# RMS normalisation of 16 x 1024 x 512 in float32: statistics computed one group ahead, and a first load begun in small transfers

## The chip, the cores and the metric

The kernel runs on one core of one Trainium2 chip. The metric is device time in microseconds (us). The profile's span of one execution is about 1.8 us shorter than that execution's device time. DVE is the vector engine, ACT the scalar engine, and SP the engine that issues the transfers; 16 DMA engines move the data, each transfer in packets. A transfer is said to have landed when the profile shows its completion; each DMA engine ends its share of a transfer with a packet of 4 bytes, the completion record. Timed comparisons were made in rounds on the same chip: the kernel before and the other kernel take turns.

## The reference, cut to what matters

```python
def reference(x, gamma):                     # x: 16 x 1024 x 512 float32
    eps = 1e-5
    rms = np.sqrt(np.mean(x ** 2, axis=-1, keepdims=True) + eps)
    return (x / rms * gamma).astype(np.float32)
```

Each of 16,384 rows of 512 numbers is read once and written once. That is 33.55 MB in and 33.55 MB out, 67.11 MB in all. No row depends on another.

## The kernel before

The rows are cut into four tiles of 128 partitions x 32 rows x 512 columns, 8.39 MB each. Three buffers ("slots") of that size lie in on-chip memory, so the fourth tile must wait until the first one has been stored. Rows are handled in groups of G = 8. ACT squares them and DVE scales them in place. For every second group DVE also sums the squares (`tensor_reduce`); for the others ACT accumulates them itself. All large transfers are issued by SP, in program order, onto one queue.

```python
    load(0, 0, 0, 16)                      # tile, slot, first row, end row
    load(0, 0, 16, 32)
    load(1, 1, 0, 32)
    ...
    def compute(slot, r0, r1):
        for g in range(r0, r1, G):
            ...
            if (g // G) % 2:
                for h in range(0, G, H):   # H = 4
                    sq = psum.tile([P, H, D], fp32, name="sq")
                    nc.scalar.activation(out=sq, in_=slots[slot][:, g + h : g + h + H, :], func=AF.Square)
                    nc.vector.tensor_reduce(out=ss[:, h : h + H], in_=sq, axis=mybir.AxisListType.X, op=OP.add)
            else:
                for r in range(G):
                    nc.scalar.activation(out=sq_scratch, in_=slots[slot][:, g + r, :],
                                         func=AF.Square, accum_out=ss[:, r : r + 1])
            nc.scalar.activation(out=rms, in_=ss, func=AF.Sqrt, bias=eps_t, scale=1.0 / D)
            nc.vector.reciprocal(out=rstd, in_=rms)
            for r in range(G):
                nc.vector.scalar_tensor_tensor(out=slots[slot][:, g + r, :], in0=slots[slot][:, g + r, :],
                    scalar=rstd[:, r : r + 1], in1=gamma_b, op0=OP.mult, op1=OP.mult)

    compute(0, 0, 8)
    store(0, 0, 0, 1)
    load(2, 2, 0, 16)
    store(0, 0, 1, 2)
    load(2, 2, 16, 24)
    store(0, 0, 2, 3)
    load(2, 2, 24, 32)
    compute(0, 8, 32)
    store(0, 0, 3, 32)
    compute(1, 0, 16)
    store(1, 1, 0, 16)
    load(3, 0, 0, 16)                      # waits until tile 0 is stored
    load(3, 0, 16, 32)
    compute(1, 16, 32)
    store(1, 1, 16, 32)
    compute(2, 0, 32)
    store(2, 2, 0, 32)
    compute(0, 0, 16)
    store(3, 0, 0, 16)
    compute(0, 16, 32)
    store(3, 0, 16, 32)
```

## Time and profile before

| | before |
|---|---|
| device time | 162.08 us, median of 3 runs (161.98 to 162.15) |
| span of the profiled execution | 161.0 us |
| DVE, ACT busy | 123.3 us, 79.9 us |
| moved by the main DMA queue | 67.11 MB |
| last store issued, landed | 148.0 us, 160.0 us |

The profiled execution itself took 162.76 us, above all the timed ones. Its trace may be trusted for what happens and in what order, but not for tenths of a microsecond.

These lines are from the profile's page of the kernel before: busy time of the engines, the 40 slices for DVE and the DMA engines, the DMA queue, and the chain that ended last, by engine.

```profile
PE 2.0 (1%) x2; PEld 0.5 (0%) x2; DVE 123.3 (77%) x163; ACT 79.9 (50%) x162; POOL 0.2 (0%) x4
...
DVE  0101909999999509999999999998999999997000
...
DMA  7999999969798999999699999999999699699993
...
q1 hardware_dynamic: 2448, 67.11, 97.4%
...
DVE 70%; ACT 12%; DMA 8%; issue 2%; DVEq 0%
```

Two readings compete here. The chain says that the vector engine bounds the kernel (70% of the span). The DMA queue says that the packets filled 97.4% of the time of all 16 DMA engines. The table of stretches speaks for the second; experiment 2 tests both. Its last two columns are the DMA share and the rate:

```profile
core 0: us, PE busy (x) PEld busy (x) DVE busy (x) ACT busy (x) POOL busy (x), PEclk, DMA share, GB/s
2.00:158.00 156.00, 2.04 (x2) 0.49 (x2) 123.12 (x161) 79.20 (x162) 0.00 (x0) 1.00 1.00 428
13.00:148.00 135.00, 0.00 (x0) 0.00 (x0) 122.43 (x160) 78.61 (x161) 0.00 (x0) 1.00 1.00 431
```

The DMA share is 1.00 for 156 of 161 us. The single digits below 9 in the DMA row need not be holes: shares of single stretches also rise above 1 (1.67 from 20 to 22 us, then 0.23 from 22 to 24), so bytes of a packet seem to be counted in one place, and only longer stretches can be trusted. The Trainium skill, "DMA: Bandwidth & Descriptors", section "Where 436 GB/s comes from", puts the ceiling of the on-chip memory's ports at 435 GB/s; the 431 GB/s of this trace are within 1% of it. "Perfetto Trace Analysis", section "Roofline", says that a core which alone uses its memory can exceed its 358 GB/s share by up to about 20%; here 431 / 358 = 1.20.

The same view restricted to single DMA issues gives the time from issue to landing. First comes the first load, then the last store, both of the kernel before. The times after "x1" are how long the issue took in ns and when it started.

```profile
L42 SPq DMA_DIRECT2D slot<-in_x_dram x1: 383/383/383, 0.7 to 0.7; - x1
...
  ACT sq_scratch L78: 10.4, 1
...
DMA to landing us min/median/max: 12.2/12.2/12.2
...
L45 SPq DMA_DIRECT2D out_dram<-slot x1: 332/332/332, 148.0 to 148.0; - x1
...
DMA to landing us min/median/max: 12.0/12.0/12.0
```

An issue takes 0.3 to 0.4 us, while its data lands 12 us later. ACT waits 10.4 us for the first load. The last store needs 4.19 MB / 431 GB/s = 9.7 us for its data alone, so at 148.0 us hardly anything was queued ahead of it: the vector engine finishes just when the stream runs dry.

These DVE lines from the timeline of the kernel before show the late start and one hole; the columns are start, duration, engine, line, operation:

```profile
24.27 10.67 DVE L87 SCALAR_TENSOR_TENSOR slot<-slot,rstd,gamma_b 128x512 f32<-128x512 f32 x16
...
60.04 0.20 DVE L85 RECIPROCAL rstd<-rms 128x8 f32<-128x8 f32 x1 [5.41 <-ACT rms L84]
```

### The profile page before, as it was taken

The page shows a single profiled execution, that of the slowest core. Times are in us where ns is not written, and L with a number is a line of the kernel's source. Part 1 is how long each engine was busy: PE and PEld are TensorE (multiplying, and loading weights), DVE is VectorE, ACT ScalarE, POOL GpSimd, SP SyncE. Part 2 cuts the span into 40 slices and gives each one's busy share as a digit, 9 for nine tenths or more (in the row PEclk, how much of TensorE's full clock was granted, in tenths as well). Part 3 has the DMA queues.
Part 4 walks back from the last instruction along what each step waited for, and adds up shares of the span by engine and source line. Part 5 has one row for each costly group of instructions (what it writes and reads, how often), then busy time and mean ns, then how long its engine had stood idle before and what let it go on. Part 6 is the DMA issues. An engine that isn't in the chain of part 4 may idle for free.

```text
span 161.0 us, 414 instructions
## 1 busy us (share of the span) xinstructions
PE 2.0 (1%) x2; PEld 0.5 (0%) x2; DVE 123.3 (77%) x163; ACT 79.9 (50%) x162; POOL 0.2 (0%) x4
## 2 busy tenths in 40 slices
PE   3100000000000000000000000000000000000000
PEld 1000000000000000000000000000000000000000
DVE  0101909999999509999999999998999999997000
ACT  3007999930490999999500933003998960000000
POOL 0000000000000000000000000000000000000000
DMA  7999999969798999999699999999999699699993
GB/s 253 399 407 497 399 423 489 521 293 489 326 466 356 466 403 501 460 472 443 297 480 407 415 480 407 407 489 407 407 497 521 277 505 521 269 489 407 407 391 138
DMA packets 2452, 67.13 MB, mean 417 GB/s; under 512 B 273, under 2 KB 273, under 8 KB 658
## 3 DMA queue, kind: packets, MB, share of 16 engines
q1 hardware_dynamic: 2448, 67.11, 97.4%
q14 instruction: 2, 0.02, 0.0%
q10 hardware_dynamic: 2, 0.00, 0.0%
HBM read 33.56 MB, written 33.55 MB: 417 GB/s over the span
## 4 chain that ended last, share of the span: by engine, by line
DVE 70%; ACT 12%; DMA 8%; issue 2%; DVEq 0%
DVE slot L87 51%; DVE ss L73 18%; DMA slot<-in_x_dram 8%; ACT sq_scratch L78 6%; ACT sq L72 4%; DVE rstd L85 1%; ACT L84 1%; ACT rms L84 1%; DVEq L142 0%
## 5 line engine op out<-in xcount | busy, mean ns | idle before, releaser
L87 DVE SCALAR_TENSOR_TENSOR slot<-slot,rstd,gamma_b 128x512 f32<-128x512 f32 x128 | 85.8, 747 | 0.1
L78 ACT ACTIVATE sq_scratch<-slot 128x512 f32<-128x512 f32 x64 | 40.1, 627 | 14.4 <-DMA slot<-in_x_dram 13.1
L73 DVE TENSOR_REDUCE ss<-sq 128x4 f32<-128x2048 f32 x16 | 36.1, 2273 | 10.3 <-ACT sq L72 10.2
L72 ACT ACTIVATE sq<-slot 128x2048 f32<-128x2048 f32 x16 | 29.8, 1865 | 13.9 <-DVE ss L73 13.9
L84 ACT ACTIVATE rms<-ss,eps_t 128x8 f32<-128x8 f32 x16 | 4.5, 298 | 27.9 <-DVE ss L73 27.7
L78 ACT ACTIVATION_READ_ACCUMULATOR sq_scratch<-slot 128x1 f32 x64 | 12.1, 189 | 0.0
L85 DVE RECIPROCAL rstd<-rms 128x8 f32<-128x8 f32 x16 | 2.9, 193 | 9.8 <-ACT rms L84 9.8
L58 DVE COPY gamma_b<-sq 128x512 f32<-128x512 f32 x1 | 0.7, 691 | 3.6 <-PE sq L56 3.6
L56 PE MATMUL sq<-gamma_row,ones_col 1*128 1x512 f32 x2 | 2.0, 1122 | 2.5 <-DMA gamma_row<-in_gamma_dram 2.5
L78 ACT ACT_TABLE_LOAD x1 | 1.3, 1283 | 1.3 <-PEq L131 1.3
L84 ACT ACT_TABLE_LOAD x1 | 1.3, 1283 | 0.0
L54 DVE MEMSET ones_col<- 1x128 f32 x1 | 0.2, 165 | 0.8 <-PEq L131 0.8
L56 PEld LDWEIGHTS sq<-gamma_row,ones_col 1*128 1x128 f32 x2 | 0.5, 305 | 2.5 <-issue 2.5
L131 POOL MEMSET const-bfloat16-1.0<- 128x1 bf16 x1 | 0.1, 103 | 0.0
L131 POOL MEMSET const-uint8-127<- 128x1 uint8 x1 | 0.1, 103 | 0.0
L131 POOL MEMSET const-float32-1.0<- 128x1 f32 x1 | 0.1, 100 | 0.0
L131 POOL MEMSET const-float32-0.0<- 128x1 f32 x1 | 0.1, 99 | 0.2 <-issue 0.2
L61 DVE MEMSET eps_t<- 128x1 f32 x1 | 0.1, 59 | 0.0
## 6 DMA issues: line engine op xcount, KB each, us to landing
slot<-in_x_dram SPq DMA_DIRECT2D x5, 4096.0 KB, 21.5
out_dram<-slot SPq DMA_DIRECT2D x4, 4096.0 KB, 16.5
out_dram<-slot SPq DMA_DIRECT2D x1, 7424.0 KB, 31.9
slot<-in_x_dram SPq DMA_DIRECT2D x2, 2048.0 KB, 34.2
out_dram<-slot SPq DMA_DIRECT2D x3, 256.0 KB, 22.8
gamma_row<-in_gamma_dram ACTq DMA_DIRECT2D x1, 2.0 KB
slot<-in_x_dram SPq DMA_DIRECT2D x1, 40.8
out_dram<-slot SPq DMA_DIRECT2D x1, 23.5
```

Of the source, the lines that this page charges most:

```text
L54: nc.vector.memset(ones_col, 1.0)
L56: nc.tensor.matmul(gamma_psum[:, 0], ones_col, gamma_row, start=True, stop=True)
L58: nc.vector.tensor_copy(out=gamma_b, in_=gamma_psum[:, 0])
L61: nc.vector.memset(eps_t, eps)
L72: nc.scalar.activation(out=sq, in_=slots[slot][:, g + h : g + h + H, :], func=AF.Square)
L73: nc.vector.tensor_reduce(out=ss[:, h : h + H], in_=sq, axis=mybir.AxisListType.X, op=OP.add)
L78: nc.scalar.activation(out=sq_scratch, in_=slots[slot][:, g + r, :], func=AF.Square, accum_out=ss[:, r : r + 1],)
L84: nc.scalar.activation(out=rms, in_=ss, func=AF.Sqrt, bias=eps_t, scale=1.0 / D)
L85: nc.vector.reciprocal(out=rstd, in_=rms)
L87: nc.vector.scalar_tensor_tensor(out=slots[slot][:, g + r, :], in0=slots[slot][:, g + r, :], scalar=rstd[:, r : r + 1], in1=gamma_b, op0=O ...
L131: nc = _bacc.Bacc("TRN2", target_bir_lowering=False, num_devices=1)
```

## The change

The intent is twofold. The statistics of group k+1 are issued before the scaling of group k, so that DVE need not wait for ACT's square root between groups. And the first 16 rows come as transfers of 2, 6 and 8 rows, so that squaring starts before all 16 have landed. (Where a text below says 2, 6, 8 and 16 rows, the 16 are the second load, which is as before.) The order of the transfers stays the same.

```diff
-    load(0, 0, 0, 16)
+    load(0, 0, 0, 2)
+    load(0, 0, 2, 8)
+    load(0, 0, 8, 16)
     load(0, 0, 16, 32)
     load(1, 1, 0, 32)
...
-    def compute(slot, r0, r1):
-        for g in range(r0, r1, G):
+    def row_stats(slot, g):          # squares, sums, square root, reciprocal of one group
...
+        return rstd
+    def apply(slot, g, rstd):        # the eight scalings of one group
...
+    groups = [(t, g) for t in range(4) for g in range(0, R, G)]
+    slot_of = [0, 1, 2, 0]
+    def transfers(t, g): ...         # the same stores and loads after the same groups as before
+    ahead = row_stats(0, 0)
+    for k, (t, g) in enumerate(groups):
+        rstd = ahead
+        if k + 1 < len(groups):
+            tn, gn = groups[k + 1]
+            ahead = row_stats(slot_of[tn], gn)
+        apply(slot_of[t], g, rstd)
+        transfers(t, g)
```

More of the change, by code (lines that the diff above doesn't have):

```diff
@@ L62 @@
     sq_scratch = const.tile([P, D], fp32)
-    def compute(slot, r0, r1):
-        for g in range(r0, r1, G):
-            ss = stats.tile([P, G], fp32, name="ss")
-            rms = stats.tile([P, G], fp32, name="rms")
-            rstd = stats.tile([P, G], fp32, name="rstd")
-            if (g // G) % 2:
-                for h in range(0, G, H):
-                    sq = psum.tile([P, H, D], fp32, name="sq")
-                    nc.scalar.activation(out=sq, in_=slots[slot][:, g + h : g + h + H, :], func=AF.Square)
-                    nc.vector.tensor_reduce(
-                        out=ss[:, h : h + H], in_=sq, axis=mybir.AxisListType.X, op=OP.add
-                    )
-            else:
-                for r in range(G):
-                    nc.scalar.activation(
-                        out=sq_scratch,
-                        in_=slots[slot][:, g + r, :],
-                        func=AF.Square,
-                        accum_out=ss[:, r : r + 1],
-                    )
-            nc.scalar.activation(out=rms, in_=ss, func=AF.Sqrt, bias=eps_t, scale=1.0 / D)
-            nc.vector.reciprocal(out=rstd, in_=rms)
-            for r in range(G):
-                nc.vector.scalar_tensor_tensor(
-                    out=slots[slot][:, g + r, :],
-                    in0=slots[slot][:, g + r, :],
-                    scalar=rstd[:, r : r + 1],
-                    in1=gamma_b,
-                    op0=OP.mult,
-                    op1=OP.mult,
-                )
@@ L96 @@
-    compute(0, 0, 8)
-    store(0, 0, 0, 1)
-    load(2, 2, 0, 16)
-    store(0, 0, 1, 2)
-    load(2, 2, 16, 24)
-    store(0, 0, 2, 3)
-    load(2, 2, 24, 32)
-    compute(0, 8, 32)
-    store(0, 0, 3, 32)
-    compute(1, 0, 16)
-    store(1, 1, 0, 16)
-    load(3, 0, 0, 16)
-    load(3, 0, 16, 32)
-    compute(1, 16, 32)
-    store(1, 1, 16, 32)
-    compute(2, 0, 32)
-    store(2, 2, 0, 32)
-    compute(0, 0, 16)
-    store(3, 0, 0, 16)
-    compute(0, 16, 32)
-    store(3, 0, 16, 32)
+    def row_stats(slot, g):
+        ss = stats.tile([P, G], fp32, name="ss")
+        rms = stats.tile([P, G], fp32, name="rms")
+        rstd = stats.tile([P, G], fp32, name="rstd")
+        if (g // G) % 2:
+            for h in range(0, G, H):
+                sq = psum.tile([P, H, D], fp32, name="sq")
+                nc.scalar.activation(out=sq, in_=slots[slot][:, g + h : g + h + H, :], func=AF.Square)
+                nc.vector.tensor_reduce(
+                    out=ss[:, h : h + H], in_=sq, axis=mybir.AxisListType.X, op=OP.add
+                )
+        else:
+            for r in range(G):
+                nc.scalar.activation(
+                    out=sq_scratch,
+                    in_=slots[slot][:, g + r, :],
+                    func=AF.Square,
+                    accum_out=ss[:, r : r + 1],
+                )
+        nc.scalar.activation(out=rms, in_=ss, func=AF.Sqrt, bias=eps_t, scale=1.0 / D)
+        nc.vector.reciprocal(out=rstd, in_=rms)
+        return rstd
@@ new lines, in apply, with transfers @@
+    def apply(slot, g, rstd):
+        for r in range(G):
+            nc.vector.scalar_tensor_tensor(
+                out=slots[slot][:, g + r, :],
+                in0=slots[slot][:, g + r, :],
+                scalar=rstd[:, r : r + 1],
+                in1=gamma_b,
+                op0=OP.mult,
+                op1=OP.mult,
+            )
+    groups = [(t, g) for t in range(4) for g in range(0, R, G)]
+    slot_of = [0, 1, 2, 0]
+    def transfers(t, g):
+        if (t, g) == (0, 0):
+            store(0, 0, 0, 1)
+            load(2, 2, 0, 16)
+            store(0, 0, 1, 2)
+            load(2, 2, 16, 24)
+            store(0, 0, 2, 3)
+            load(2, 2, 24, 32)
+        elif (t, g) == (0, 24):
+            store(0, 0, 3, 32)
+        elif (t, g) == (1, 8):
+            store(1, 1, 0, 16)
+            load(3, 0, 0, 16)
+            load(3, 0, 16, 32)
+        elif (t, g) == (1, 24):
+            store(1, 1, 16, 32)
+        elif (t, g) == (2, 24):
+            store(2, 2, 0, 32)
+        elif (t, g) == (3, 8):
+            store(3, 0, 0, 16)
+        elif (t, g) == (3, 24):
+            store(3, 0, 16, 32)
```

## The prediction

> **What bounds the kernel now.** The page's chain of waits names the vector engine (70% of the span), and its first piece is 12.2 us of waiting for the first load. I do not believe it. The DMA lines say that queue q1 moved 67.11 MB and its packets filled 97.4% of 16 engines' span. In the table of stretches the DMA share is 1.00 from 2 to 158 us (428 GB/s) and from 13 to 148 us (431 GB/s). The Trainium skill, "DMA: Bandwidth & Descriptors", section "Where 436 GB/s comes from", gives 435 GB/s as the ceiling of the 16 SBUF ports; the trace agrees within 1%. The vector engine merely finishes just in time: the last store is issued at 148.0 us and lands 12.0 us later, of which 4.19 MB at 431 GB/s are 9.7 us. From the other end: 67.11 MB / 431 GB/s = 155.7 us, plus 1.7 us before the first packet and about 1 us after the last: nearly 160 of the 161 us.
>
> **What the change does.**
> - It removes no bytes and no compute: 128 scalings of 747 ns, 16 reductions of 2273 ns, the same ACT work.
> - The first load becomes transfers of 2, 6 and 8 rows. Squares start when 0.52 MB has landed, about 4 us instead of 12.97 us. Rows 2-8 arrive by about 8 us; with 0.74 us a row and a 1.28 us table load, the first scaling starts near 14.3 us instead of 24.27.
> - Statistics one group ahead keep reductions off the path between groups; the 5.4 us hole of the vector engine at 55-60 us should mostly go. But later tiles' data come when they did (the last load near 111.5 us). I estimate the last store issued at 138 to 144 us instead of 148.0.
> - Cost: two more DMA issues (about 0.4 us each on the idle SP queue) and 16 more descriptors per DMA engine. A 32 KB packet takes 1.213 us and a 64 KB one 2.418, so a packet's fixed part is about 8 ns: 0.15 us in all.
>
> **How much is on the critical path.** All transfers go through one SP queue in the same program order, the queue never empty: earlier stores wait behind queued loads. The only slack near the end: most engines idle for some 0.6 us around 148.5 us, until the last store's first packet; the slowest engine (it ends about 1 us after the rest) does not. So the gain is 0 to 0.6 us, the cost about 0.15 us: net nothing.
>
> **Prediction:** 162.1 us, 8 in 10 between 161.7 and 162.7. Faster by over 2%: 0.01; within 2%: 0.97; slower: 0.02.
>
> **What would show each step.** Right: DMA share stays 1.00 between 2 and 158 us at about 428 GB/s; the first scaling starts near 14 us; the last vector instruction ends 4 to 10 us earlier; and the last store's time to landing grows by as much, from 12.0 to 16-22 us. Last load and last store land when they did. Wrong: the first packets leave a hole in the DMA share in the first 10 us, or any hole later.
>
> **What would make it wrong.** The small first transfers starving the engines before the next issue; a slower DMA rate when loads' landing semaphores are reused; a start of the first packets that is faster for small transfers (gain up to 0.5 us); or a new order in which a store comes too late for the queue.

## The result, and the profile after

| | before | after |
|---|---|---|
| device time, median | 162.05 us (161.86 to 162.15, 6 runs) | 162.42 us (162.29 to 162.58, 6 runs) |
| ratio, after / before | | 1.0025, 95% interval 1.0012 to 1.0038 |
| first scaling on DVE starts | 24.27 us | 14.96 us |
| last store issued | 148.0 us | 142.6 us |
| last store landed | 160.0 us | 159.7 us |

A ratio here is the mean time of one kernel's runs over that of the other's in the same rounds, so it is not quite the ratio of the quoted medians. The small difference of 0.37 us is a loss that is clear of noise.

The same lines of the page, after:

```profile
PE 2.0 (1%) x2; PEld 0.5 (0%) x2; DVE 122.5 (76%) x163; ACT 80.0 (50%) x162; POOL 0.2 (0%) x4
...
DVE  0103999999994199999999999999999999940000
...
DMA  5999999979799999998899999999999699699992
...
q1 hardware_dynamic: 2736, 67.11, 97.5%
...
DVE 51%; DMA 25%; ACT 10%; issue 1%; SPq 1%; DVEq 0%
```

DVE starts some slices earlier and stops two slices earlier. The DMA row is as full as before. The queue shows 288 packets more, for the same bytes. The stretches after:

```profile
2.00:158.00 156.00, 2.04 (x2) 0.50 (x2) 122.34 (x161) 79.27 (x162) 0.00 (x0) 1.00 1.00 430
13.00:148.00 135.00, 0.00 (x0) 0.00 (x0) 121.65 (x160) 73.01 (x146) 0.00 (x0) 1.00 1.00 431
```

The share and the rate are unchanged. The first load (now two rows) and the last store, after:

```profile
L42 SPq DMA_DIRECT2D slot<-in_x_dram x1: 383/383/383, 0.7 to 0.7; - x1
...
  ACT sq_scratch L79: 2.3, 1
...
DMA to landing us min/median/max: 4.1/4.1/4.1
...
L45 SPq DMA_DIRECT2D out_dram<-slot x1: 332/332/332, 142.6 to 142.6; - x1
...
DMA to landing us min/median/max: 17.1/17.1/17.1
```

ACT's first wait fell from 10.4 to 2.3 us. The last store is issued 5.4 us earlier and takes 5.1 us longer to land, because it now stands behind others in the queue. That is where the gain went: it became waiting time of a store. The same DVE lines, after, and one of ACT that precedes the second:

```profile
14.96 4.07 DVE L91 SCALAR_TENSOR_TENSOR slot<-slot,rstd,gamma_b 128x512 f32<-128x512 f32 x6
...
42.69 0.63 ACT L79 ACTIVATE sq_scratch<-slot 128x512 f32<-128x512 f32 x1 [7.84 <-DMA slot<-in_x_dram]
...
55.68 0.20 DVE L86 RECIPROCAL rstd<-rms 128x8 f32<-128x8 f32 x1 [5.64 <-ACT rms L85]
```

The hole in the second tile did not go away. It moved from 54.6-60.0 us to 50.0-55.7 us and is as long as before. The line of ACT shows why the new order could not close it: ACT had waited 7.84 us for the second tile, could start on it only at 42.69 us (42.44 us before), and then squared without a pause until the square root at 55.35 us.

### The profile page after: what moved, and what is told of

It reads as the page before. It is cut to its first block, busy times and chain, and to the rows that moved or that the text cites. A ratio compares the mean times of both kernels' runs of the same rounds, so it can differ in the third digit from the quotient of the medians.

```text
span 160.8 us, 420 instructions
## 1 busy us (share of the span) xinstructions
PE 2.0 (1%) x2; PEld 0.5 (0%) x2; DVE 122.5 (76%) x163; ACT 80.0 (50%) x162; POOL 0.2 (0%) x4
## 4 chain that ended last, share of the span: by engine, by line
DVE 51%; DMA 25%; ACT 10%; issue 1%; SPq 1%; DVEq 0%
DVE slot L91 38%; DMA slot<-in_x_dram 25%; DVE ss L74 12%; ACT sq_scratch L79 5%; ACT sq L73 4%; SPq L42 1%; DVE rstd L86 1%; ACT rms L85 1%; DVEq L159 0%
```

## The experiments

Twelve kernels were run, in three groups of four; each group shared one chip and its runs of the kernel before. The main theory (A) is that the DMA stream never empties, so earlier compute buys only slack, and the 0.37 us come from the split load. The rivals are that the vector chain bounds the kernel, that the new order itself costs the time (B), or that it gains and the split gives the gain back (C).

### 1. Each half of the change alone

`order_only` takes the changed kernel with the loads of before:

```diff
-    load(0, 0, 0, 2)
-    load(0, 0, 2, 8)
-    load(0, 0, 8, 16)
+    load(0, 0, 0, 16)
```

> The new order of statistics with the two 16-row loads of before. Theory A (the DMA stream is never empty, so only the stream's own cost counts, and the +0.37 us come from the split load): 0.0 us against before, within 0.15, although the last store is issued 4 to 6 us earlier. Rival B (the new order costs the time, for instance by stores that wait longer in the queue): +0.3 to +0.4 us. Rival C (the order gains and the split gives it back): -0.3 us or more.

`split_only` makes the opposite edit in the kernel before.

> The order of before, with the first load split 2, 6, 8, 16. Theory A: +0.37 us against before (0.2 to 0.5), as the whole change. Rival B: 0.0. Rival C: more than +0.6 us.

| | median | ratio to before (median 162.15 us), 95% interval |
|---|---|---|
| order_only | 161.96 us | 0.9992 (0.9978 to 1.0006) |
| split_only | 162.62 us | 1.0025 (1.0011 to 1.0038) |

The order does nothing to the time, and the split alone loses as much as the whole change (0.25%). Rivals B and C fall. Both halves moved the last store forward: from 148.0 us to 146.5 us (order) and to 144.1 us (split), together to 142.6 us. The earlier start gives more of the slack than the new order does: order_only moved the last store by 1.5 us, not by the 4 to 6 us expected. Yet that was enough to close the one gap in the stream. Between 147 and 150 us the time in which DMA engines had no packet in hand is 0.40 us per engine in the trace of the kernel before and 0.00 in that of order_only. The time did not fall, and the packets show a likely reason: in the kernel before, the engine that ended last finished its data at 159.65 us and all others by 158.70 us. Its last eight packets of 1.213 us reach back to about 150 us, so it was probably still busy with earlier packets when the others ran dry.

### 2. Is the slack real, and is the vector engine a bound?

`before_plus` and `after_plus` add six scalings into an unused scratch tile ahead of the last group's scaling:

```diff
+    for r in range(6):               # last group of the last tile only
+        nc.vector.scalar_tensor_tensor(out=idle_out, in0=slots[slot][:, g + r, :],
+            scalar=rstd[:, r : r + 1], in1=gamma_b, op0=OP.mult, op1=OP.mult)
```

> The kernel before, with six more scalings of 0.74 us (results to a scratch tile) in the vector engine's last group: 4.4 us of vector work. In the kernel before the last store is issued at 148.0 us, just as the queue runs dry. Theory A (the DMA stream is the bound, and the vector engine of before has no slack left at the end): the last store is issued near 152.4 us and lands 11 to 12 us later: +3.5 to +4.4 us. A rival by which the vector engine has slack: 0.

> The same six scalings in the changed kernel. Theory A (the change bought slack at the end, about 5.5 us, and no time): the last store is issued near 147.0 us, still ahead of the stream: +0.4 us against before, as the change without them. A rival by which the chain through the vector engine bounds the kernel: +4.4 us on top of the change, +4.8 us in all.

`one_stat` takes the changed kernel and uses the first group's statistics for all rows. Its result is wrong (relative error 0.04).

```diff
-        if k + 1 < len(groups):
-            tn, gn = groups[k + 1]
-            ahead = row_stats(slot_of[tn], gn)
```

> The changed kernel with the statistics of the first group alone, used for all rows (a wrong result on purpose): all 16 reductions, 36 us of vector work, and 15/16 of the squares go; transfers and scalings stay. Theory A (DMA bound): 162.4 us, +0.2 to +0.5 us against before. The rival that reads the page's chain (vector engine 51% to 70% of the span): 10 to 35 us faster.

| | median | ratio to before (median 162.18 us), 95% interval |
|---|---|---|
| before_plus | 165.93 us | 1.0234 (1.0220 to 1.0249) |
| after_plus | 162.88 us | 1.0047 (1.0034 to 1.0060) |
| one_stat | 162.88 us | 1.0051 (1.0029 to 1.0073) |

The last store of before_plus, then of after_plus:

```profile
L45 SPq DMA_DIRECT2D out_dram<-slot x1: 333/333/333, 151.8 to 151.8; - x1
...
DMA to landing us min/median/max: 11.1/11.1/11.1
```

```profile
L45 SPq DMA_DIRECT2D out_dram<-slot x1: 333/333/333, 146.6 to 146.6; - x1
...
DMA to landing us min/median/max: 13.1/13.1/13.1
```

In before_plus the store comes too late and the stream runs dry: 151.8 + 11.1 = 162.9 us, and the kernel loses 3.75 us. In after_plus the store is issued 4.0 us later than in the changed kernel and lands at the same 159.7 us (146.6 + 13.1, against 142.6 + 17.1). The slack that the change bought is real and swallows the extra work.

The page of one_stat:

```profile
PE 2.0 (1%) x2; PEld 0.5 (0%) x2; DVE 86.1 (54%) x132; ACT 8.6 (5%) x19; POOL 0.2 (0%) x4
...
q1 hardware_dynamic: 2736, 67.11, 97.5%
```

ACT's work fell from 80.0 to 8.6 us and DVE's from 122.5 to 86.1 us, and the kernel is not faster at all. The page's chain, which put DVE at 70% and 51%, is thereby refuted as a statement of what would make the kernel faster: order_only and split_only free DVE earlier in the kernel before without a gain, and one_stat takes work away in the changed kernel without one. It does not follow that DVE had slack in the kernel before. There both end together, and before_plus shows that added vector work at the end costs time.

Both kernels with the split are above what was expected (0.7 us between the medians, where +0.4 us and +0.2 to +0.5 us were expected). For after_plus the spans settle most of it: they are 0.35 us longer than those of the kernel before, as the change alone would make them, and the rest lies outside the span, where before_plus also has 0.3 us more (3.4 of its 3.75 us are in the span). For one_stat all 0.8 us (mean) lie in the span, its runs spread from 162.28 to 163.63 us, and the cause stays open.

### 3. What does the split cost, and why more than its packets?

A 32 KB packet takes 1.213 us and a 64 KB one 2.418 us, so a packet's fixed part is 2 x 1.213 - 2.418 = 0.008 us. The split adds 16 packets and two completion records of 9 ns per engine: 0.15 us. The measured loss is 0.37 us. Four kernels ask whether the rest belongs to the start of the stream.

`start_8x2` and `mid_8x2` are the kernel before with rows 0 to 15, or rows 16 to 31, of the first tile as eight transfers of two rows:

```diff
-    load(0, 0, 0, 16)
+    for r in range(0, 16, 2):        # mid_8x2: the second load, range(16, 32, 2)
+        load(0, 0, r, r + 2)
```

> The order of before, rows 0 to 15 of the first tile in eight transfers of two rows, at the start of the stream: 56 more descriptors per DMA engine (7 transfers, 8 each) at 8.5 ns and 7 completions at 9 ns are +0.54 us. Theory A with a start effect (small packets also lose time while the stream starts up, about 0.25 us): +0.8 us. Rival D (descriptors alone): +0.54 us.

> The same eight transfers of two rows, but for rows 16 to 31, when the stream is already running: the same 56 descriptors and 7 completions. Theory A with a start effect: +0.54 us, 0.2 to 0.3 us less than the split at the start. Rival D: the same as the split at the start.

| | median | ratio to before (median 162.15 us), 95% interval |
|---|---|---|
| start_8x2 | 162.55 us | 1.0033 (1.0012 to 1.0053) |
| mid_8x2 | 163.00 us | 1.0052 (1.0039 to 1.0064) |

start_8x2 lost 0.54 us, which is what rival D has for the packets alone, and 0.3 us less than a start effect would give; that mid_8x2 lost more, neither theory expected. But mid_8x2 was a flawed test: its last store was issued at 149.4 us, after the stream had run dry, because the kernel before has no slack at the end. So it was repeated in the new order, which has 1.5 us of it, and the change's own split of 2, 6 and 8 rows was moved to rows 16 to 31:

```diff
     load(0, 0, 0, 16)
-    load(0, 0, 16, 32)
+    load(0, 0, 16, 18)               # mid_8x2_ahead: eight transfers of two rows
+    load(0, 0, 18, 24)
+    load(0, 0, 24, 32)
```

> The new order (slack at the end), rows 0 to 15 whole, and the same split of 2, 6 and 8 rows for rows 16 to 31, where the stream already runs: as many descriptors more as in the change. Theory E (the split costs more than its descriptors only at the start of the stream): 0.0 to +0.15 us against before. Rival F (it costs the same anywhere): +0.37 us.

> The split of rows 16 to 31 into eight transfers of two rows again, now in the new order. In the first try the last store was issued at 149.4 us, after the queue had run dry, so its +0.85 us hold vector work too. Descriptors alone: +0.45 to +0.55 us against before; if they cost more than counted, again +0.85 us.

| | median | ratio to before (median 162.22 us), 95% interval |
|---|---|---|
| mid_268_ahead | 162.14 us | 0.9998 (0.9985 to 1.0011) |
| mid_8x2_ahead | 162.33 us | 1.0025 (0.9999 to 1.0051) |

The change's split costs 0.25% at the start of the stream and nothing measurable one transfer later. That supports theory E, though the two were measured on different chips, each against its own runs of the kernel before. mid_8x2_ahead was flawed as mid_8x2 was: its last store was issued at 148.2 us, and its DMA engines had no packet for 0.43 us each between 147 and 150 us.

Do the traces show a mechanism? In the kernel order_only the packets that start in the first 4 us take 0.60 us per engine longer, in sum, than the usual duration of their size. In the changed kernel the packets of 4 and 12 KB, which land in its first 8 us, take 0.86 us longer. The difference of 0.26 us and the 0.15 us of added packets make 0.41 us, against 0.37 us measured, but this sum leaves out the rest of the stream. Packets that start between 36 and 42 us, where loads turn to stores, lose 0.49 us in order_only and 0.13 us in the changed kernel. Over all packets of the queue a DMA engine is busy for 156.81 us in order_only, 156.84 us in the changed kernel and 156.73 us in split_only. So the packet times do not show where the loss arises.

What they show, in one execution each, is when the engines end. On average an engine's last data packet ends at 158.17 us in order_only and at 158.31 us in the changed kernel, later by about the 0.15 us of the added packets; for the engine that ends last, and so ends the kernel, it is 159.04 and 159.40 us. Why that engine loses more than the others stays open, and so does why packets are slow at the start.

The eight-transfer pair does not confirm theory E: start_8x2 (+0.33%) and mid_8x2_ahead (+0.25%) overlap, and the packets' own 0.54 us (0.33%) are enough for either. Theory E rests on the 2-6-8 pair of times alone. A rival was not tested: that any rearrangement of the transfers can shift the time by some 0.4 us. half_second below, with 0.08 us of added packets, is 0.24% slower.

### 4. Can the stream itself be made cheaper?

If only the stream counts, fewer transfers should gain. `merged` drops the three one-row stores and loads the third tile whole, right after the second, in the new order:

```diff
     load(1, 1, 0, 32)
+    load(2, 2, 0, 32)
...
-        if (t, g) == (0, 0):
-            store(0, 0, 0, 1)
-            load(2, 2, 0, 16)
-            ...
-        elif (t, g) == (0, 24):
-            store(0, 0, 3, 32)
+        if (t, g) == (0, 24):
+            store(0, 0, 0, 32)
```

> Candidate: the new order, the two 16-row loads of before, the third tile loaded whole right after the second, and the first tile stored whole. Three one-row stores and two loads fewer: 40 descriptors per DMA engine (8.5 ns each) and 5 completions (9 ns) less. Theory A (the stream's own cost is all that counts, and the new order's slack suffices): -0.38 us against before, between -0.2 and -0.5. A rival by which such small terms do not add up in the stream: 0.

`merged_halves` is the same with `load(1, ...)` and `load(2, ...)` in halves of 16 rows; `half_second` is order_only with `load(1, ...)` alone in halves.

> The new order, two 16-row loads of the first tile, and the second tile's load in two halves (32 KB packets instead of 64 KB). In the traces the last 64 KB packets before the first store took 0.4 to 0.5 us longer per engine. Theory G (large packets stretch at that turn): -0.2 to -0.3 us against before. Rival: 8 more descriptors per engine, +0.08 us, so 0.0 within noise.

> The merged candidate (no one-row stores, third tile loaded at once), but every early load in 16-row halves: 24 descriptors per engine and 3 completions less than in the kernel before. Theory G: -0.2 to -0.4 us against before. Rival (a long run of loads itself is slower, whatever the packets): +0.2 to +0.4 us, as the merged candidate.

| | median | ratio to before, 95% interval |
|---|---|---|
| merged | 162.55 us | 1.0030 (1.0015 to 1.0045) |
| half_second | 162.62 us | 1.0024 (1.0006 to 1.0041) |
| merged_halves | 163.48 us (162.14 to 164.02) | 1.0072 (1.0043 to 1.0102) |

merged was timed on another chip than the other two (medians of the kernel before: 162.18 and 162.22 us). merged and half_second missed both of the values written down for them. merged_halves lost, as its rival had it, but by more (+1.2 us between the means) than the +0.2 to +0.4 us expected. Theory G falls with half_second. In merged, the second tile's load was issued at 1.64 us and landed 40.2 us later, and the third's was issued at 2.11 us and landed 60.1 us later. So the third tile took 20.4 us for 8.39 MB, where 431 GB/s make 19.5. The loss shows in the last packets before the first store: those that start between 58 and 60 us take 0.6 us per engine longer than usual in merged, and 0.8 us in merged_halves. In the kernel before, the packets at that turn (38 us) lose about 0.4 us. It looks as if a longer run of loads loses more where it turns to stores. That is an observation from single traces, and its cause stays open. No kernel beats the kernel before outside its interval.

## Why the prediction was right

- **The bound.** It put the DMA stream before the page's chain and said that the vector engine "merely finishes just in time". one_stat shows the first, in the changed kernel: 36 us of vector work and 71 us of ACT work fewer, and no gain. before_plus shows the second: no slack at the end of the kernel before.
- **The compute moves.** First scaling near 14.3 us: measured 14.96. Last store at 138 to 144 us: 142.6. Its time to landing 16 to 22 us: 17.1. DMA share 1.00 between 2 and 158 us at about 428 GB/s: 1.00 and 430.
- **The gain goes into slack.** before_plus and after_plus show it from both sides: the same 4.4 us of work cost 3.75 us before, and in the changed kernel left the last landing at 159.7 us.
- **The time.** 162.1 us (161.7 to 162.7) was predicted, and 162.42 us was measured.
- **Mis-sized: the cost.** "16 more descriptors per DMA engine ... 0.15 us in all" counted a packet's fixed part alone. The loss measured 0.37 us between the medians (0.25%, and 0.25% in split_only), more than double. In the traces the average DMA engine ends later by about 0.15 us, as predicted; the engine that ends last ends 0.36 us later, and the prediction has no term for that. The cause stays open. The prediction's possible gain at the start ("a start of the first packets that is faster for small transfers") had the wrong sign: the first packets lost 0.26 us more than whole ones.
- **Wrong: the hole.** "The 5.4 us hole of the vector engine at 55-60 us should mostly go." A hole of 5.64 us stands at 50.0-55.7 us in its place, again in front of a reciprocal that waits for ACT's square root. The step that failed is the wait: the hole was put down to the order of the statistics, but in the changed kernel ACT was waiting for the second tile's rows, which let it start at 42.69 us. The hole cost no time, since the last store was issued 5.4 us earlier all the same.
- **The gain of 0 to 0.6 us at the end** did not appear: order_only, which keeps the loads of before, is at 0.9992 with 1 inside the interval. The prediction had named the reason, that the slowest engine has no gap there; experiment 1 has the numbers that fit it. Gain and cost did not cancel to "net nothing": the gain was about 0 and the cost 0.37 us, and the time stayed in the range because both are small.

## What to carry to other kernels

When the DMA share is 1.00 from the first packet to the last, shortening an engine's chain of waits, however long, need not gain anything; take that engine's work away once, and if the time stays, reordering compute can only buy slack. Add work at the end too: here the kernel before had no slack there (3.75 us lost for 4.4 us of work), though its DMA share was 1.00. To see where a gain in compute went, compare the last store's issue time and its time to landing: one falling while the other grows by as much is slack. A split of the first transfer to start compute sooner is worth making only if the kernel waits for that compute at the end; in this saturated stream it cost 0.25%.

## What the Trainium skill lacked or had wrong

- "DMA: Bandwidth & Descriptors", section "Where 436 GB/s comes from": it says that for transfers between HBM and on-chip memory the HBM side (about 358 GB/s) binds. This single-core stream, half loads and half stores, ran at 431 GB/s for 135 us, at the port ceiling. The sentence lacks the condition that the page on traces cited above gives, that only one core uses the memory.
- "DMA: Bandwidth & Descriptors", section "Rules for kernel authors": it says to coalesce many small transfers into one large one. The run merged, with five transfers fewer, was 0.30% slower, not faster. That does not contradict the rule: the smallest transfers joined here were of 256 KB, and merged also moved the third tile's load ahead of the first stores. The page has nothing on a long run of loads that loses 0.6 to 0.8 us where it turns to stores.
- None of the pages read has that the first packets of a stream are slow, by 0.5 to 0.9 us per engine in sum. Nor have they that splitting the first transfer cost 0.25% of the time and the same split one transfer later nothing measurable (0.9998); the cause of this is open.
- "Perfetto Trace Analysis", section "Identifying the Most-Contended Engine": it says to judge DMA by the rate against the memory's peak and not by occupancy. Here both agree (120% of 358 GB/s, 97.4% occupancy). It lacks the case that misled here: a chain of releases puts an engine at 51% of the span (in the changed kernel) whose work can be cut by 36 us without a gain, as one_stat shows.
